# A two-layer encoder trunk on one core: one sigmoid, the heads' weight rests and x1's transposes put in a given order, x1's first tile scaled out of its PSUM bank, and half of tiles three and four scaled by ScalarE

## The chip, the cores and the metric

The program runs on one core of a Trainium2 chip. A core has five engines that this text speaks of: TensorE (PE in the profile; PEld is its weight load), VectorE (DVE), ScalarE (ACT), GpSimd (POOL) and SyncE (SP), which here only issues DMAs. Each engine takes its instructions in the order in which they were written into its queue; they wait for one another by semaphores. The metric is the device time of one execution in microseconds, less is better. The kernel before takes 660.94 us, the median of 3 runs (660.82 to 661.03).

## The reference

The trunk has two layers over 512 tokens of width 1024. Cut to what matters here:

```python
def rmsnorm(x, g):
    y = x * lax.rsqrt(jnp.mean(x * x, axis=-1, keepdims=True) + EPS)
    return y * g

for i in range(2):
    xn = rmsnorm(x, norm_g[i])
    y = mixer_na(xn, ...) if i == 0 else mixer_mla(xn, ...)
    h = x + y
    gate = jax.nn.sigmoid(rmsnorm(h, ple_norm[i]) @ ple_w_gate[i])
    x = h + gate * (p[i] @ ple_w_proj[i])
return rmsnorm(x, final_norm)
```

`mixer_na` is neighbourhood attention over a token grid. `mixer_mla` projects xn to a compressed query `c_q` (384 columns), a compressed key and value `c_kv` (256) and a rotary key part (32), normalises both, widens them to 16 heads of 96 query and key columns (64 without position, 32 rotary) and 64 value columns, and attends densely. Both mixers are multiplied by a SiLU gate before their output projection.

## The kernel before

Tokens lie in four tiles of 128 rows, t = 0 to 3; a tile has two halves of 512 columns, n (or g) = 0 and 1. Every fp32 product is made of three matmuls: each operand is split into a rounded main part ("hi") and the rest ("lo"), and hi·hi, lo·hi and hi·lo are added. For a weight, ScalarE makes the main part with a copy (`whi`, `wwhi`) and GpSimd the rest by a subtraction (`wlo`, `wwlo`; lines 83, 84, 583, 585); the raw weight comes by a DMA from SyncE's queue into one of three buffers (`wraw`). For an activation, ScalarE copies the transposed tile out of PSUM and VectorE subtracts (`split`, lines 94 and 96).

The program is written as one stream of calls. A scheduler of the compiler gives each engine its order by a timeline of its own, as far as data allows; `self.tc.issue_after(ins)` holds the instructions of a block behind `ins` where both are on the same engine, and adds no wait between engines.

Two stretches matter.

**From layer 0's gate to layer 1's compression.** `gate_seven` computes the gate product as seven block products instead of eight (block order 1, 7, 2, 6, 5, 3, 4; `p` in the code), each of two times 12 matmuls (i = 0, 1). Several products use one PSUM bank one after another: 6, 5 and 3 add up in a bank of tag T, 7 and 4 in one of tag S. After 6, ScalarE copies the bank to `s6` (L649 `s`), before 5 may add to it. `finish` applies the sigmoid (L592), multiplies by the projected embedding `pe` (L600) and adds to the residual tile `res[t]` (L602, `r`). Product 2 finishes tiles 0 and 1, half 0; 5 finishes tiles 2 and 3, half 1; 3 finishes tiles 0 and 1, half 1; 4 finishes tiles 2 and 3, half 0. Then `done` runs for the half: sum of squares (L1057), mean `mn` (L1058), and, once both halves are there, `rs` = mean^-0.5 on GpSimd (L1063), x1's scaling r · rs · gn on VectorE (L1071, `x1n`; gn is the norm's gain), four transposes a half on TensorE (L139), and the split into `x1h` and `x1l`. `mla_c` multiplies x1's tiles by the compression weights: part 0 with 384 columns, part 1 with 288, each in four chunks of k, 24 matmuls a tile and part (L107), and copies the results out (L685, `c`).

**The heads of layer 1.** `mla_heads` runs 64 steps of scores; the pair of heads j takes eight steps. For the next pairs it prepares rotary queries every second pair: `rope` ends with the main part `rh` (ScalarE, L771) and the rest `rl` (GpSimd, L772), which DMAs of SyncE's queue move into the query tiles `qe` and `qo`. GpSimd also normalises each step's exponentials (L830, `ex`) and makes the rests of the weights to come.

Of the kernel before, what the change touches and what calls it, by code (L numbers as in the profile page):

```python
# [16 lines left out]
ALU = mybir.AluOpType  # L17
# [3 lines left out]
S = 512  # L21
# [19 lines left out]
class Trunk:  # L41
# [522 lines left out]
    def gate_seven(self, pool, layer, rh, res, after):  # L564
# [22 lines left out]

        behind, loaded = [], self.last_load

        def finish(t, n, ps, o=0, wd=S, last=False):  # L590
# [10 lines left out]
            r = res[t][:, n * S + o:n * S + o + wd]  # L601
            (nc.vector if last else nc.gpsimd).tensor_tensor(out=r, in0=r, in1=x, op=ALU.add)  # L602
            if layer == 0 and last and (t, n) not in ((0, 0), (1, 0)):
                after(t, n, o, wd)
            else:
                behind.append(lambda: after(t, n, o, wd))
# [12 lines left out]
        for k, p in enumerate(order):  # L619
# [7 lines left out]
            for i in range(2):  # L627
                for o, wd in halves if i and p in (7, 4) else ((0, S),):
                    c = slice(o, o + wd)
                    if p in banks:  # L630
# [3 lines left out]
                         for c in range(2) for s, r in ((0, 0), (1, 0), (0, 1)) for k in (2 * c, 2 * c + 1)]  # L634
                    for j, (l, r) in enumerate(m):
                        with self.tc.issue_after(mm.ins):
                            mm = nc.tensor.matmul(ps, l, r, start=j == 0 and p in banks,  # L637
                                                  stop=j == 11 and p in (2, 3, 4), skip_group_check=True)
# [8 lines left out]
                    elif p == 6:  # L647
                        s6[i] = self.temp("s6")
                        copy = nc.scalar.activation(s6[i], ps, AF.Copy)  # L649
                        if i:  # L650
                            prep(order[-1], copy)
# [3 lines left out]
                    elif p == 5:  # L655
                        q = self.psum("mm" if i else "T")
                        sub(q, ps, s17[i])
                        sub(ps, ps, s1[i])
                        finish(2 + i, 1, q, last=layer == 0)
                    elif p == 2:  # L660
                        finish(i, 0, ps, last=True)
                    elif p == 3:
                        finish(i, 1, ps, last=True)
                    else:
                        finish(2 + i, 0, ps, o, wd, True)
# [3 lines left out]
    def mla_c(self, pool, xT, cT, sets):  # L669
# [47 lines left out]
    def mla_heads(self, pool, xT, cT, sets, oT):  # L717
# [32 lines left out]
        def load_qr(g, after=None):  # L750
            load(("qr", g), a["mla_qr"][g], 384, after)

# [103 lines left out]
        def pieces(j):  # L856
# [87 lines left out]
    def run(self):  # L944
# [64 lines left out]
        for layer in range(2):  # L1009
            with tc.tile_pool(name=f"out{layer}", bufs=4, reuse_waits="tile") as pool:  # L1010
# [38 lines left out]
                if layer == 0:  # L1049
                    mean = {}  # L1050

                    def done(t, n, o, w):
# [4 lines left out]
                        nc.scalar.activation(sq, r[:, n * S:(n + 1) * S], AF.Square, accum_out=ss)  # L1057
# [5 lines left out]
                        nc.gpsimd.tensor_tensor(out=rs, in0=mn, in1=self.half, op=ALU.pow)  # L1063
                        nc.gpsimd.tensor_scalar(self.rows[1][0][:, t:t + 1], mn, 1.0, None, op0=ALU.add)
                        nc.sync.dma_start(self.spill[t], r)
                        if not x1T:
                            x1T.extend([[self.bigtile(f"x1{s}{g}") for g in range(2)] for s in "hl"])
                        xn = pool.tile([P, D], F32, name="x1n", tag="xn", bufs=2)
                        for g in range(2):
                            c = slice(g * S, (g + 1) * S)  # L1070
                            nc.vector.scalar_tensor_tensor(xn[:, c], r[:, c], rs, gn[:, c], op0=ALU.mult, op1=ALU.mult)  # L1071
# [148 lines left out]
```

## Time and profile before

| what | us |
|---|---|
| median of 3 runs | 660.94 |
| the profiled execution's own time | 660.64 |
| its span in the trace | 658.4 |
| PE busy | 647.0 (98%) |
| POOL busy | 432.7 (66%) |
| ACT busy | 439.1 (67%) |
| DVE busy | 402.1 (61%) |

Times in the trace count from the start of the span. A busy PE is not PE at its peak, since matmuls overlap and their ends are modelled; what a stretch takes is better read from the starts of its instructions. In the rows of a timeline the columns are start, length, engine, line, operation, out<-in, shape and count, and in brackets how long the engine had been idle and for whom.

### The profile page before, as it was taken

The page shows a single profiled execution, that of the slowest core. Times are in us where ns is not written, and L with a number is a line of the kernel's source. Part 1 is how long each engine was busy: PE and PEld are TensorE (multiplying, and loading weights), DVE is VectorE, ACT ScalarE, POOL GpSimd, SP SyncE. Part 2 cuts the span into 40 slices and gives each one's busy share as a digit, 9 for nine tenths or more (in the row PEclk, how much of TensorE's full clock was granted, in tenths as well). Part 3 has the DMA queues.
Part 4 walks back from the last instruction along what each step waited for, and adds up shares of the span by engine and source line. Part 5 has one row for each costly group of instructions (what it writes and reads, how often), then busy time and mean ns, then how long its engine had stood idle before and what let it go on. Part 6 is the DMA issues. An engine that isn't in the chain of part 4 may idle for free.

```text
span 658.4 us, 10122 instructions
## 1 busy us (share of the span) xinstructions
PE 647.0 (98%) x3419; PEld 550.6 (84%) x3419; DVE 402.1 (61%) x856; ACT 439.1 (67%) x875; POOL 432.7 (66%) x381
## 2 busy tenths in 40 slices
PE   9999999999999999999999999999999999999994
PEld 6888888998988888887899888888888888888884
DVE  6290365845656516568834613888888886474855
ACT  7672586767767743787543635897979897537945
POOL 0495475895685673787554526785959878436974
PEclk9999999999999999999999999999999999999998
DMA  9944354987575989444733334120212213583524
GB/s 320 354 143 147 98 198 122 250 221 166 190 175 181 199 192 348 157 155 158 246 86 118 103 102 148 53 76 6 64 52 66 66 65 128 205 306 128 171 86 159
DMA packets 44755, 102.18 MB, mean 155 GB/s; under 512 B 4640, under 2 KB 17696, under 8 KB 44704
## 3 DMA queue, kind: packets, MB, share of 16 engines
q1 hardware_dynamic: 33776, 83.97, 38.0%
q0 software_dynamic: 10496, 16.78, 11.7%
q10 hardware_dynamic: 432, 0.79, 0.3%
q8 instruction: 27, 0.44, 0.3%
q14 instruction: 24, 0.20, 0.1%
HBM read 89.99 MB, written 25.17 MB: 175 GB/s over the span
## 4 chain that ended last, share of the span: by engine, by line
PE 92%; DVE 2%; ACT 2%; DMA 1%; issue 1%; POOL 1%; POOLq 0%; ACTq 0%
PE ps_mm L107 35%; PE ps_S L107 13%; PE ps_mm L734 7%; PE ps_T L139 6%; PE ps_O L845 5%; PE ps_T L637 4%; PE ps_T L107 3%; PE ps_O L107 3%; PE ps_T L238 2%; PE ps_O L400 2%; PE ps_S L637 2%; PE ps_mm L637 2%; PE ps_mm L184 2%; PE ps_T L388 2%; PE ps_S L352 1%; PE ps_S L351 1%
## 5 line engine op out<-in xcount | busy, mean ns | idle before, releaser
L84 POOL TENSOR_TENSOR wwlo<-wraw,wwhi 128x1024 fp32r<-128x1024 f32 (+5 forms) x78 | 143.3, 1852 | 74.7 <-ACT wwhi L83 53.2
L83 ACT ACTIVATE wwhi<-wraw 128x1024 fp32r<-128x1024 f32 (+5 forms) x81 | 65.5, 832 | 57.3 <-issue 19.2
L585 POOL TENSOR_TENSOR wlo<-wraw,whi 128x512 fp32r<-128x512 f32 x56 | 74.0, 1356 | 24.7 <-ACT whi L583 14.9
L830 POOL TENSOR_TENSOR ex<-ex,rc 128x512 f32<-128x512 f32 x64 | 66.1, 1043 | 25.1 <-DVE rc L829 18.1
L828 ACT ACTIVATE ex<-ps_S,mx 128x512 f32<-128x512 f32 x64 | 44.0, 687 | 12.1 <-DVE mx L826 11.1
L826 DVE TENSOR_REDUCE mx<-ps_S 128x1 f32<-128x512 f32 x64 | 43.7, 682 | 7.1 <-PE ps_S L107 6.5
L96 DVE TENSOR_TENSOR pt_lo<-ps_T,pt_hi 128x512 fp32r<-128x512 f32 x64 | 43.2, 681 | 7.6 <-ACT pt_hi L94 7.3
L374 POOL TENSOR_TENSOR ex<-ex,rc 128x128 f32<-128x128 f32 (+1 forms) x64 | 36.0, 619 | 15.0 <-DVE rc L370 15.0
L94 ACT ACTIVATE pt_hi<-ps_T 128x512 fp32r<-128x512 f32 x64 | 37.7, 594 | 4.2 <-PE ps_T L139 3.9
L107 PE MATMUL ps_mm<-xh,wwhi 128*128 128x512 f32 x152 | 40.3, 398 | 0.0
L107 PE MATMUL ps_mm<-xl,wwhi 128*128 128x512 f32 x152 | 38.4, 391 | 0.0
L139 PE MATMUL ps_T<-ident,ex 128*128 128x128 f32 x256 | 38.4, 272 | 0.0
L107 PE MATMUL ps_mm<-xh,wwlo 128*128 128x512 f32 x152 | 38.2, 391 | 0.0
L139 PEld LDWEIGHTS ps_T<-ident,ex 128*128 128x128 f32 x256 | 31.4, 140 | 7.7 <-POOL ex L830 0.4
L107 PEld LDWEIGHTS ps_mm<-xh,wwlo 128*128 128x128 f32 x152 | 28.3, 188 | 5.9
L107 PEld LDWEIGHTS ps_mm<-xl,wwhi 128*128 128x128 f32 x152 | 28.3, 188 | 5.7
L583 ACT ACTIVATE whi<-wraw 128x1024 fp32r<-128x1024 f32 x28 | 29.2, 1055 | 4.9 <-DMA wraw<-sum 2.7
L205 DVE TENSOR_TENSOR u<-ps_O,u 64x512 f32<-64x512 f32 x32 | 22.0, 687 | 17.2 <-ACT u L204 16.7
L368 ACT ACTIVATE ex<-ex,mx 128x128 f32<-128x128 f32 (+1 forms) x64 | 30.3, 476 | 2.7 <-DVE mx L358 1.8
L209 POOL TENSOR_TENSOR u<-u,z 128x512 f32<-128x512 f32 x16 | 21.9, 1368 | 15.2 <-DVE u L205 10.0
L107 PEld LDWEIGHTS ps_mm<-xh,wwhi 128*128 128x128 f32 x152 | 27.3, 188 | 4.8
L107 PE MATMUL ps_S<-ke,qe 96*128 96x512 f32 x96 | 29.0, 408 | 0.3 <-DMA qe<-rl 0.3
(432 smaller groups left out, 1847.0 us busy)
## 6 DMA issues: line engine op xcount, KB each, us to landing
sum<-gate POOLq DMA_DIRECT2D x12, 1024.0 KB, 8.2
wraw<-na_qk SPq DMA_DIRECT2D x16, 512.0 KB, 3.3
wraw<-sum SPq DMA_DIRECT2D x16, 512.0 KB, 3.3
pe<-pe SPq DMA_DIRECT2D x31, 256.0 KB, 6.4
wraw<-gate SPq DMA_DIRECT2D x12, 512.0 KB, 3.3
wraw<-na_v SPq DMA_DIRECT2D x8, 512.0 KB, 4.1
sum<-sum POOLq DMA_DIRECT2D x4, 1024.0 KB, 10.7
wraw<-na_o SPq DMA_DIRECT2D x8, 512.0 KB, 4.4
```

Source lines behind the costliest of these rows:

```text
L83: nc.scalar.activation(hi[:, c], raw[:, c], AF.Copy)
L84: f = lambda e, c=c: e.tensor_tensor(out=lo[:, c], in0=raw[:, c], in1=hi[:, c].bitcast(F32), op=ALU.subtract)
L94: self.last_copy = nc.scalar.activation(hi, src, AF.Copy, scale=scale)
L96: nc.vector.tensor_tensor(out=lo, in0=src, in1=hi.bitcast(F32), op=ALU.subtract)
L107: last = self.last_mm = nc.tensor.matmul(out, l, r, start=i == 0, stop=i == n - 1)
L139: self.last_mm = self.nc.tensor.transpose(t[:, i * P:(i + 1) * P], b, self.ident)
L585: nc.gpsimd.tensor_tensor(out=lo[:, o], in0=raw[:, o], in1=hi[:, o].bitcast(F32), op=ALU.subtract)
L637: mm = nc.tensor.matmul(ps, l, r, start=j == 0 and p in banks, stop=j == 11 and p in (2, 3, 4), skip_group_check=True)
L734: self.last_mm = nc.tensor.matmul(PS[key], *terms[i], start=i == 0, stop=i == len(terms) - 1)
L826: nc.vector.reduce_max(mx, sp, axis=AX.X, negate=True)
L828: nc.scalar.activation(ex, sp, AF.Exp, bias=mx, accum_out=sm)
L830: nc.gpsimd.tensor_tensor(out=ex, in0=ex, in1=rc.to_broadcast([P, S]), op=ALU.mult)
```

## The change

- In `gate_seven`, the finish of product 2's second tile (t = 1, half 0) is kept back until ScalarE has copied product 6's first bank to `s6`. Before, its sigmoid could stand ahead of that copy.
- For tile 0, half 1, VectorE's last add of `finish` writes to the PSUM bank instead of to `r`. The squares and the scaling read that bank; ScalarE copies it to `r` for the spill to memory. Half 0 of tile 0 is multiplied by the gain on VectorE early, and ScalarE applies `rs` to it.
- For tiles 2 and 3, half 1 is multiplied by the gain on GpSimd (`xg`) as soon as it is there, and ScalarE applies `rs`.
- x1's transposes get fixed places in TensorE's queue: tile 0's eight ahead of the last six matmuls of product 4, tile t+1's ahead of the second half of tile t's matmuls of part 0. GpSimd's rest of part 0's third weight chunk is put behind tile 0's `rs`.
- In `mla_heads`, the rests of the next rotary query weights, and in one pair those of the embedding `pT`, are put behind `rl` of the pair on GpSimd.

```diff
-        behind, loaded = [], self.last_load
+        behind, kept, loaded = [], [], self.last_load
...
-            (nc.vector if last else nc.gpsimd).tensor_tensor(out=r, in0=r, in1=x, op=ALU.add)
+            held = ps if layer == 0 and (t, n) == (0, 1) else r
+            (nc.vector if last else nc.gpsimd).tensor_tensor(out=held, in0=r, in1=x, op=ALU.add)
             if layer == 0 and last and (t, n) not in ((0, 0), (1, 0)):
-                after(t, n, o, wd)
+                after(t, n, o, wd, held)
...
+                        if layer == 0 and (p, i, j) == (4, 1, 6):
+                            mm = self.turned[0]
                         with self.tc.issue_after(mm.ins):
...
                         copy = nc.scalar.activation(s6[i], ps, AF.Copy)
+                        if kept:
+                            with self.tc.issue_after(copy.ins):
+                                finish(*kept.pop(), last=True)
...
+                    elif p == 2 and i and layer == 0:
+                        kept.append((i, 0, ps))
...
-            ws = [self.load_w(a["mla_c"][part][c], 2 * wn, extra=c == 3) for c in range(4)]
+            ws = []
+            for c in range(4):
+                with self.tc.issue_after(self.power.ins) if (part, c) == (0, 2) else nullcontext():
+                    ws.append(self.load_w(a["mla_c"][part][c], 2 * wn, extra=c == 3))
...
-                self.mms(ps[:, :wn], self.by_chunk(lambda s, k: L(xT[s], k, t), W))
+                m = self.by_chunk(lambda s, k: L(xT[s], k, t), W)
+                for j, (l, r) in enumerate(m):
+                    with self.tc.issue_after(self.turned[t + 1].ins) if (part, j) == (0, 12) and t < 3 else nullcontext():
+                        mm = nc.tensor.matmul(ps[:, :wn], l, r, start=j == 0, stop=j == 23)
...
-        def load(key, ap, n, after=None):
+        def load(key, ap, n, after=None, rests=None):
             with self.tc.issue_after((A.get(after) or self.last_copy).ins) if after else nullcontext():
-                W_[key] = self.load_w(ap, n, parts=2)
+                with self.tc.issue_after(A[rests].ins) if rests else nullcontext():
+                    W_[key] = self.load_w(ap, n, parts=2)
...
-                add(2, *((load_qr, g + 1, ("q", n)) if j < 5 else (load, "p", a["pT"][1], 1024, ("q", n))))
+                add(2, *((load_qr, g + 1, ("q", n), ("rl", g)) if j < 5 else
+                         (load, "p", a["pT"][1], 1024, ("q", n), ("rl", g))))
...
+                        half = r[:, n * S:(n + 1) * S] if held is None else held
+                        nc.scalar.activation(sq, half, AF.Square, accum_out=ss)
                         if t not in mean:
                             mean[t] = mn
+                            if t > 1:
+                                ahead[t, n] = self.temp("xg")
+                                nc.gpsimd.tensor_tensor(out=ahead[t, n], in0=r[:, n * S:(n + 1) * S],
+                                                        in1=gn[:, n * S:(n + 1) * S], op=ALU.mult)
                             return
...
+                        if t == 0:
+                            self.power = power
...
+                        if t == 0:
+                            nc.scalar.activation(r[:, S:], half, AF.Copy)
...
+                        if t == 0:
+                            ahead[t, 0] = xn[:, :S]
+                            nc.vector.tensor_tensor(out=xn[:, :S], in0=r[:, :S], in1=gn[:, :S], op=ALU.mult)
                         for g in range(2):
                             c = slice(g * S, (g + 1) * S)
-                            nc.vector.scalar_tensor_tensor(xn[:, c], r[:, c], rs, gn[:, c], op0=ALU.mult, op1=ALU.mult)
+                            if (t, g) in ahead:
+                                nc.scalar.activation(xn[:, c], ahead[t, g], AF.Copy, scale=rs)
+                            else:
+                                nc.vector.scalar_tensor_tensor(xn[:, c], r[:, c] if t else half, rs, gn[:, c],
+                                                               op0=ALU.mult, op1=ALU.mult)
...
+                        self.turned[t] = self.last_mm
```

The scheduler makes these orders of it. On TensorE, from the last 18 matmuls of product 4 (`ps_S<-..,X`) into part 0 of the compression (`ps_mm<-..,x1h` and `x1l`), the queue before and then now:

```order
L637 MATMUL ps_S<-whi,X_2977 128x512 x4
L637 MATMUL ps_S<-wlo,X_2977 128x512 x2
L637 MATMUL ps_S<-whi,X_2977 128x512 x4
L637 MATMUL ps_S<-wlo,X_2977 128x512 x2
L139 MATMUL ps_T<-ident,x1n 128x128 x12
L107 MATMUL ps_mm<-wwhi,x1h_3364 128x384 x4
L139 MATMUL ps_T<-ident,x1n 128x128 x4
L107 MATMUL ps_mm<-wwhi,x1l_3366 128x384 x2
```

```order
L640 MATMUL ps_S<-whi,X_2977 128x512 x4
L640 MATMUL ps_S<-wlo,X_2977 128x512 x2
L139 MATMUL ps_T<-ident,x1n 128x128 x8
L640 MATMUL ps_S<-whi,X_2977 128x512 x4
L640 MATMUL ps_S<-wlo,X_2977 128x512 x2
L698 MATMUL ps_mm<-wwhi,x1h_3369 128x384 x2
L698 MATMUL ps_mm<-wwhi,x1l_3371 128x384 x2
L698 MATMUL ps_mm<-wwlo,x1h_3369 128x384 x2
```

Tile 0's eight transposes moved ahead of six matmuls of product 4, and no transposes stand between a tile's first `x1h` matmuls and its `x1l` matmuls there.

On GpSimd, in the same place (`wlo`: product 4's weights; `wwlo`: part 0's; `rs`: tile 0's power first), before and then now:

```order
L585 TENSOR_TENSOR wlo<-wraw,whi 128x512 x14
L84 TENSOR_TENSOR wwlo<-wraw,wwhi 128x768 x3
L1063 TENSOR_TENSOR rs<-mn,half 128x1
L1064 TENSOR_SCALAR rowa_80<-mn 128x1
L1063 TENSOR_TENSOR rs<-mn,half 128x1
```

```order
L585 TENSOR_TENSOR wlo<-wraw,whi 128x512 x14
L84 TENSOR_TENSOR wwlo<-wraw,wwhi 128x768
L1080 TENSOR_TENSOR xg<-r,gn 128x512
L84 TENSOR_TENSOR wwlo<-wraw,wwhi 128x768
L1080 TENSOR_TENSOR xg<-r,gn 128x512
L1084 TENSOR_TENSOR rs<-mn,half 128x1
L1087 TENSOR_SCALAR rowa_80<-mn 128x1
L84 TENSOR_TENSOR wwlo<-wraw,wwhi 128x768
```

One weight rest left the front of tile 0's `rs`, and two multiplications by the gain came to stand there.

On SyncE, the moves of the last pairs' rotary queries (`mla_o` is a weight of the output projection), before and then now:

```order
L101 DMA qe_3528<-rh 32x512
L82 DMA wraw<-mla_o 128x1024
L101 DMA qo_3530<-rh 32x512
L101 DMA qe_3521<-rl 32x512
L101 DMA qo_3523<-rl 32x512
```

```order
L101 DMA qe_3534<-rh 32x512
L101 DMA qe_3527<-rl 32x512
L101 DMA qo_3529<-rl 32x512
L101 DMA qe_3535<-rl 32x512
L101 DMA qo_3536<-rh 32x512
```

The first move of `rl` went ahead of the weight and of a move of `rh`.

More of the change, by code (lines that the diff above doesn't have):

```diff
@@ L743, in k_terms, with load_qr @@
             return [(W(r, k), (ch, cl)[s][:, 3 + k, :]) for s, r in ((0, 0), (1, 0), (0, 1)) for k in range(2)]
-        def load(key, ap, n, after=None):
+        def load(key, ap, n, after=None, rests=None):
             with self.tc.issue_after((A.get(after) or self.last_copy).ins) if after else nullcontext():
-                W_[key] = self.load_w(ap, n, parts=2)
-        def load_qr(g, after=None):
-            load(("qr", g), a["mla_qr"][g], 384, after)
+                with self.tc.issue_after(A[rests].ins) if rests else nullcontext():
+                    W_[key] = self.load_w(ap, n, parts=2)
+        def load_qr(g, after=None, rests=None):
+            load(("qr", g), a["mla_qr"][g], 384, after, rests)
         def load_kv(g, after=None):
@@ L1049, in run, with done @@
                 if layer == 0:
-                    mean = {}
-                    def done(t, n, o, w):
+                    mean, ahead, self.turned = {}, {}, {}
+                    def done(t, n, o, w, held=None):
                         r = res[t]
@@ L1056, in done @@
                         mn = self.small.tile([P, 1], F32, name="mn", tag="mn")
-                        nc.scalar.activation(sq, r[:, n * S:(n + 1) * S], AF.Square, accum_out=ss)
+                        half = r[:, n * S:(n + 1) * S] if held is None else held
+                        nc.scalar.activation(sq, half, AF.Square, accum_out=ss)
                         nc.vector.tensor_scalar(mn, ss, 1.0 / D, mean.get(t, EPS), op0=ALU.mult, op1=ALU.add)
@@ L1060, in done @@
                             mean[t] = mn
+                            if t > 1:
+                                ahead[t, n] = self.temp("xg")
+                                nc.gpsimd.tensor_tensor(out=ahead[t, n], in0=r[:, n * S:(n + 1) * S],
+                                                        in1=gn[:, n * S:(n + 1) * S], op=ALU.mult)
                             return
                         rs = self.small.tile([P, 1], F32, name="rs", tag="rs")
-                        nc.gpsimd.tensor_tensor(out=rs, in0=mn, in1=self.half, op=ALU.pow)
+                        power = nc.gpsimd.tensor_tensor(out=rs, in0=mn, in1=self.half, op=ALU.pow)
+                        if t == 0:
+                            self.power = power
                         nc.gpsimd.tensor_scalar(self.rows[1][0][:, t:t + 1], mn, 1.0, None, op0=ALU.add)
+                        if t == 0:
+                            nc.scalar.activation(r[:, S:], half, AF.Copy)
                         nc.sync.dma_start(self.spill[t], r)
```

## The prediction

> **What bounds the kernel.** I read the page first, then TensorE's waits, then the timelines of every engine around the few places where TensorE stood still.
>
> ```profile
> PE 647.0 (98%) x3419; PEld 550.6 (84%) x3419; DVE 402.1 (61%) x856; ACT 439.1 (67%) x875; POOL 432.7 (66%) x381
> ```
>
> TensorE's queue is the bound. The change removes no matmul, so it can gain only where TensorE waits. The waits that the change touches, the last of them at a weight load (total, times, longest):
>
> ```profile
> PE ps_T L637 <- ACT s L649: 0.6, 1, 0.6
> ...
> PE ps_mm L107 <- ACT x1h L94: 0.4, 1, 0.4
> ...
> PEld ps_S L107 <- DMA qe<-rl: 1.0, 2, 0.8
> ```
>
> The view counts only gaps between modelled ends, so I take each loss from the starts in TensorE's timeline:
>
> ```profile
> 304.43 0.61 PE L637 MATMUL ps_T<-wlo,X 128*128 128x512 f32 x2
> 305.66 1.20 PE L637 MATMUL ps_T<-whi,X 128*128 128x512 f32 x4 [0.61 <-ACT s L649]
> ...
> 320.75 1.07 PE L637 MATMUL ps_S<-whi,X 128*128 128x512 f32 x4
> ...
> 322.12 1.47 PE L139 MATMUL ps_T<-ident,x1n 128*128 128x128 f32 x12
> 323.55 0.62 PE L107 MATMUL ps_mm<-wwhi,x1h 128*128 128x384 f32 x2
> ...
> 332.26 0.62 PE L107 MATMUL ps_S<-wwhi,x1h 128*128 128x384 f32 x2
> ...
> 343.53 0.43 PE L107 MATMUL ps_T<-wwhi,x1h 128*128 128x288 f32 x2
> ...
> 356.09 0.81 PE L139 MATMUL ps_T<-ident,cn 128*128 128x128 f32 x6
> ```
>
> and the pace of undisturbed work from the chain of waits:
>
> ```profile
> 316.83 5.46 PE ps_S L637 x24
> ...
> 325.57 5.56 PE ps_mm L107 x32
> ...
> 356.25 0.66 PE ps_T L139 x6
> ```
>
> A 512-column matmul takes 5.46/24 = 0.2275 us, a 384-column one 5.56/32 = 0.174, a transpose 0.66/6 = 0.11. From these, the three losses:
>
> Loss 1, the `s` copy: after 304.43 two matmuls are due to end at 304.885, and product 5 starts at 305.66: 0.775 us.
>
> Loss 2, x1's transposes: from 322.12 to 343.53 are 21.41 us for 32 transposes and 96 matmuls of part 0, 32 x 0.11 + 96 x 0.174 = 20.2: 1.2 us. From 343.53 part 1 runs at an even pace.
>
> Loss 3 is in the heads:
>
> ```profile
> 517.91 0.71 PE L107 MATMUL ps_S<-ke,qe 96*128 96x512 f32 x2
> 518.97 0.50 PE L107 MATMUL ps_S<-ke,qe 96*128 96x512 f32 x1 [0.34 <-DMA qe<-rl]
> 519.30 0.40 PE L734 MATMUL ps_mm<-cT,wwhi 128*128 128x512 f32 x1
> ...
> 525.85 0.95 PE L107 MATMUL ps_S<-ke,qe 96*128 96x512 f32 x3
> 526.63 1.09 PE L734 MATMUL ps_mm<-cT,wwhi 128*128 128x512 f32 x4
> ```
>
> A step's three score matmuls behind transposes take 0.78 us (525.85 to 526.63), here 1.39: 0.61 us. The other of the two weight-load waits is 1.0 - 0.8 = 0.2 us, at an earlier pair; I count half of it. Together 0.7. All that the change can win is 0.775 + 1.2 + 0.7 = 2.7 us.
>
> **The sigmoid.** ScalarE's queue ahead of product 5:
>
> ```profile
> 303.61 0.64 ACT L592 ACTIVATE ps_mm<-ps_mm,rs 128x512 f32<-128x512 f32 x1
> 304.40 0.63 ACT L1057 ACTIVATE sq<-r 128x512 f32<-128x512 f32 x1
> ...
> 305.03 1.06 ACT L649 ACTIVATE s<-ps_T 128x512 f32<-128x512 f32 x2
> ```
>
> Both `s` copies stood behind the sigmoid and a square, though product 6's first bank was ready 12 x 0.2275 = 2.7 us before 304.9. Now the first copy takes the place at 303.61 and ends near 304.2, 0.7 ahead of need. The second follows sigmoid and square at about 305.3 to 305.9; product 5's second half needs it 2.7 us after 304.9. So 0.775 is won whole, and everything on TensorE to product 4 moves forward by as much. The price is a sigmoid later by half a microsecond, and one multiplication more on VectorE (x1n from r and gn, near 305). Each is hidden: VectorE's next work for TensorE is on product 5's first bank, which ends near 307.9. Bounds of the term: 0 if another operand came last, 0.775; I take 0.775.
>
> **x1's first tile.** The eight transposes now stand where the row at 320.75 stood, which becomes 320.75 - 0.775 = 319.98: 2.1 us sooner than 322.12. Both halves of x1n must be there by then, or everything behind in TensorE's queue waits, product 4's last six matmuls too. When are they? GpSimd first:
>
> ```profile
> 307.17 5.05 POOL L585 TENSOR_TENSOR wlo<-wraw,whi 128x512 fp32r<-128x512 f32 x4 [3.25 <-issue]
> 312.19 3.66 POOL L84 TENSOR_TENSOR wwlo<-wraw,wwhi 128x768 fp32r<-128x768 f32 x2
> 316.73 1.84 POOL L84 TENSOR_TENSOR wwlo<-wraw,wwhi 128x768 fp32r<-128x768 f32 x1 [0.88 <-ACT wwhi L83]
> 318.53 0.55 POOL L1063 TENSOR_TENSOR rs<-mn,half 128x1 f32<-128x1 f32 x1
> ```
>
> The chain to 312.19 stays, since it hangs on ScalarE's copies behind the second `s`, which move little. Then come two weight rests (3.66) and two `xg`. No GpSimd product r·gn is in the trace; the nearest row is its 128x512 operation on three SBUF tiles in `rope`:
>
> ```profile
> L770 POOL TENSOR_TENSOR rl<-rh,rl x4: 1289/1296/1306, 402.7 to 508.1; 128x512 f32<-128x512 f32 x4
> ```
>
> Two at about 1.27: 312.19 + 3.66 + 2.54 = 318.4, then `rs` ends at 318.95. That is as late as before (318.53 + 0.55 = 319.08), because two `xg` cost what one weight rest and its wait did. The bounds of an `xg` are 1.02 (half of the two `ex` in a row below) and 1.84 (a longer weight rest), so `rs` could end between 318.5 and 320.1.
>
> ScalarE then scales half 0. Ahead of it stands product 4's first sigmoid:
>
> ```profile
> 315.81 0.85 ACT L83 ACTIVATE wwhi<-wraw 128x768 fp32r<-128x768 f32 x1 [0.36 <-DMA wraw<-mla_c]
> ...
> 317.18 0.64 ACT L592 ACTIVATE ps_T<-ps_T,rs 128x512 f32<-128x512 f32 x1
> ...
> 322.32 0.66 ACT L592 ACTIVATE ps_S<-ps_S,rs 128x512 f32<-128x512 f32 x1 [1.69 <-PE ps_S L637]
> ```
>
> The sigmoid at 322.32 began 0.2 us after product 4 left TensorE at 322.12. The first half of product 4 ends 320.75 - 6 x 0.2275 - 0.775 = 318.6, its sigmoid runs 318.8 to 319.45, and the scaling, about 0.63 like the square above, ends near 320.05. Half 1 is scaled on VectorE out of PSUM. In front of it, ScalarE's copy to `r` (0.53, half of the two `s` above) pushes the sigmoid of 317.18 to 317.7; it ends at 318.35. VectorE multiplies, adds and scales, 0.7 to 0.75 each as in the `x1n` row below, to 320.5. The transposes of half 1 are due at 319.98 + 0.44 = 320.42. So tile 0 is late by about 0.1 us, and `rs` has half a microsecond of slack in front of ScalarE.
>
> **The later tiles.** With the transposes from 320.1, tile 0's part 0 begins at 320.1 + 0.88 + 6 x 0.2275 = 322.35. I carried each engine's new order forward, with about 0.6 us for ScalarE's and 0.7 us for VectorE's operations on 512 columns. Tile 0's `x1l` half 0 is ready near 322.4 (needed 322.7). GpSimd's third weight rest ends near 320.95, `rs` of tile 1 at 322.45, x1n of tile 1 at 323.85 (needed 324.4 for half 0, 324.9 for half 1). Tile 2 is ready at 325.9 (needed 326.35); its second transposes need the bank that VectorE leaves at 327.05 (needed 327.1). Tile 3 is ready at 329.2, needed 332.4. The fourth weight chunk is copied near 334.9 (needed 336.7). The slacks are 0.05 to 0.5 us, so I charge 0.15 for all later tiles beside the 0.1 for tile 0: of 1.2 us, 0.95 is won. Part 1 and the z products behind it keep their operands early: their weight copies hang on TensorE itself, and move with it.
>
> A price for going wrong here: VectorE's scaling meets GpSimd on the same memory.
>
> ```profile
> L1071 DVE SCALAR_TENSOR_TENSOR x1n<-r,rs,gn 128x512 f32<-128x512 f32 x8 | 5.6, 747 | 0.0
> ...
> L128 DVE SCALAR_TENSOR_TENSOR cn<-c,rs,gq 128x384 f32<-128x384 f32 x1 | 1.8, 1847 | 0.7 <-POOL rs L123 0.7
> ```
>
> The same operation with fewer elements took 1.85 instead of 0.75 us beside GpSimd's weight rests. Tile 0's half 1 now comes from PSUM; tile 1 has both tensor inputs in SBUF, but its `rs` stands behind the third weight rest on GpSimd, which is then idle, so I charge nothing. If it met one, x1n of tile 1 would come 1.1 us later, 0.6 beyond its slack. [...]
>
> **The heads.** GpSimd and SyncE ahead of the wait at 518.97:
>
> ```profile
> 510.37 2.55 POOL L84 TENSOR_TENSOR wwlo<-wraw,wwhi 128x512 fp32r<-128x512 f32 x2
> 512.88 2.04 POOL L830 TENSOR_TENSOR ex<-ex,rc 128x512 f32<-128x512 f32 x2
> 514.87 1.30 POOL L772 TENSOR_TENSOR rl<-rl,rh 128x512 fp32r<-128x512 f32 x1
> ```
>
> ```profile
> 514.17 0.63 SPq L101 DMA_DIRECT2D qe<-rh  x1
> 514.89 0.53 SPq L82 DMA_DIRECT2D wraw<-mla_o  x1
> 516.08 0.51 SPq L101 DMA_DIRECT2D qo<-rh  x1
> 516.69 0.54 SPq L101 DMA_DIRECT2D qe<-rl  x1
> ```
>
> Without the two weight rests ahead of it, `rl` ends by about 514.1 instead of 516.2 (the second `ex` waits for its reciprocal, so 2.1 is won rather than 2.55). `qe<-rl` now follows the row at 514.17 directly: 514.89 instead of 516.69, so it lands 1.8 us sooner, against the 0.61 missing. The wait goes, and 0.7 is won with the smaller one. The price: the two rests (2.55) run after `rl`, to 516.65, and the `ex` behind them begins half a microsecond later than the 516.17 at which `rl` ended before. A step's `ex` is transposed three steps after its scores (`turn(i - 3)`), which covers that; without this cover TensorE would lose the half microsecond. `mla_o` and `pT` come later by a few DMAs, far from their use.
>
> **The sum.** 0.775 + 0.95 + 0.7 = 2.4 us. The profiled execution took 660.64 for a span of 658.4, its median stands 0.3 above it at 660.94. So the changed kernel should come out at 660.94 - 2.4 = 658.5 us.
>
> **Rivals.**
>
> *A, late tiles.* The fixed places of the transposes cost what they free: TensorE reaches each tile before its x1n, by 0.2 to 0.5 us at a time (the slacks above are that small). Then loss 2 stays, and 0.775 + 0.7 remain: 659.5. Against it: VectorE and ScalarE idle at these places in the carried order.
>
> *B, the heads only pay elsewhere.* `rl` is early but another move or a late `ex` holds the scores, and only the gate's end gains: 660.94 - 1.7 = 659.2. Against it: the 1.8 us against 0.61.
>
> *C, nothing.* Product 5 waits for another operand and the tiles are late: within 0.2% (1.3 us, about what a measurement here tells from no change), near 660.4.
>
> *D, slower.* Tile 0's transposes, put into the middle of product 4, stop TensorE until `rs` is there. Tile 3's last sigmoid, `rs` and x1n come from the matmuls behind them, so a stall is not made up. Every us by which `rs` ends beyond 319.4 is lost whole; from 2.4 on the gain is gone, from 3.7 it is slower by 0.2%. That needs two `xg` of 2.5 us and more, or a third weight chunk that arrives as late. With both `xg` at the upper bound (1.84) the loss is 0.7, which gives 659.2; a loss of 4.5 would give 663.
>
> **Chances.** My forecast 0.55 (its own range 658.0 to 659.0), A 0.18, B 0.08, C 0.1, D 0.09. Faster by more than 1.3 us are the forecast, B and nearly all of A: 0.79; same 0.12; slower 0.09. The range runs from 657.7 (all 2.7 us won, and half a microsecond of spread) to 660.5; above it lie D and a little of C.
>
> **What would show it.** Right: no wait of product 5 for the `s` copy; about 34.4 us from tile 0's first transposes to those of `cn` (32 x 0.11 + 6 x 0.2275 + 96 x 0.174 + 12.56 + 0.25); no wait for `qe<-rl`. Wrong: a gap ahead of the transposes of x1n with GpSimd's `rs` or ScalarE's scaling as its end; a wait of part 0 for `x1l`; a score waiting for `qe` or transposes waiting for `ex` after 510.

## The result and the profile after

The changed kernel takes 657.94 us, the median of 6 runs (657.81 to 658.27); the kernel before took 660.98 beside it (660.81 to 661.04). The ratio is 0.9955 with a 95% interval of 0.9943 to 0.9968: 3.0 us faster, by the interval 2.1 to 3.8. The profiled execution took 657.81 us for a span of 655.9, 2.5 us less than the span before.

The page's busy times, and the waits of TensorE (whole span) and of its weight load (290 to 600 us), in the kernel after:

```profile
PE 646.3 (99%) x3419; PEld 551.1 (84%) x3419; DVE 399.5 (61%) x854; ACT 441.6 (67%) x879; POOL 433.9 (66%) x383
...
PE ps_T L972 <- PEq L1242: 0.8, 1, 0.8
...
PEld ps_T L640 <- ACT X L533: 0.5, 1, 0.5
PEld ps_T L139 <- ACT x1n L1100: 0.5, 1, 0.5
PEld ps_T L640 <- DVE X L534: 0.4, 1, 0.4
```

The same matmuls run, and the three waits that the prediction named are gone; what the first view has left is the wait at the kernel's start. One new row stands at the weight load: x1's transposes wait for ScalarE's scaling.

TensorE's timeline at the rows that answer to those of before (start of product 5 and its next block, tile 0's transposes, part 1's first matmuls, `cn`'s transposes):

```profile
304.41 0.62 PE L640 MATMUL ps_T<-wlo,X 128*128 128x512 f32 x2
304.87 1.07 PE L640 MATMUL ps_T<-whi,X 128*128 128x512 f32 x4
...
306.23 1.07 PE L640 MATMUL ps_T<-whi,X 128*128 128x512 f32 x4
...
319.38 0.61 PE L640 MATMUL ps_S<-wlo,X 128*128 128x512 f32 x2
320.02 1.09 PE L139 MATMUL ps_T<-ident,x1n 128*128 128x128 f32 x8
...
341.71 0.43 PE L698 MATMUL ps_T<-wwhi,x1h 128*128 128x288 f32 x2
...
354.48 0.82 PE L139 MATMUL ps_T<-ident,cn 128*128 128x128 f32 x6
```

Product 5 starts 0.79 us sooner, with no gap. One block of six matmuls further on it is 0.92 us ahead, since the kernel before took longer for the first block behind its wait (305.66 to 307.15, 1.49 us) than the kernel after (1.36):

```profile
307.15 1.07 PE L637 MATMUL ps_T<-whi,X 128*128 128x512 f32 x4
```

Tile 0's transposes were due two matmuls behind 319.38, at 319.835, and start 0.185 late. Part 1 of the compression starts 1.82 us sooner (341.71; before: 343.53), and `cn` is reached 1.61 us sooner.

The other engines there (ScalarE, then VectorE, then GpSimd):

```profile
303.56 0.58 ACT L652 ACTIVATE s<-ps_T 128x512 f32<-128x512 f32 x1
...
305.22 0.59 ACT L652 ACTIVATE s<-ps_T 128x512 f32<-128x512 f32 x1
...
319.25 0.71 ACT L1100 ACTIVATE x1n<-x1n,rs 128x512 f32<-128x512 f32 x1
```

```profile
318.95 0.74 DVE L1102 SCALAR_TENSOR_TENSOR x1n<-ps_T,rs,gn 128x512 f32<-128x512 f32 x1
```

```profile
316.77 1.30 POOL L1080 TENSOR_TENSOR xg<-r,gn 128x512 f32<-128x512 f32 x1
318.01 0.57 POOL L1084 TENSOR_TENSOR rs<-mn,half 128x1 f32<-128x1 f32 x1
```

The first `s` copy ends at 304.14, 0.7 us ahead of need. `rs` ends at 318.58, half 1 is scaled by 319.69 and half 0 by 319.96: it is ScalarE's half that holds the transposes.

The heads, at the place of the old wait for `qe<-rl` (TensorE, GpSimd, SyncE):

```profile
516.23 0.94 PE L107 MATMUL ps_S<-ke,qe 96*128 96x512 f32 x3
517.01 0.39 PE L748 MATMUL ps_mm<-cT,wwhi 128*128 128x512 f32 x1
```

```profile
511.28 1.30 POOL L787 TENSOR_TENSOR rl<-rl,rh 128x512 fp32r<-128x512 f32 x1
512.53 2.55 POOL L84 TENSOR_TENSOR wwlo<-wraw,wwhi 128x512 fp32r<-128x512 f32 x2
```

```profile
512.16 0.53 SPq L101 DMA_DIRECT2D qe<-rh  x1
512.79 0.54 SPq L101 DMA_DIRECT2D qe<-rl  x1
```

The three scores take 0.78 us instead of 1.39, the two weight rests follow `rl`, and `qe<-rl` is issued right behind `qe<-rh`.

**Where the time came from.** A start of the timeline says by how much TensorE is ahead of the kernel before. Profiled executions are shifted against each other by up to 0.4 us from their start on; I take the row `ps_mm<-wlo,X` at 294.28 (before) as zero and subtract its shift (after: 294.26, so 0.02). The table gives the lead in us so worked out, at `cn`'s transposes (before: 356.09), at the matmuls of `cT` behind the scores that wait for `qe<-rl` (481.23 and 519.30), at a product of the projected embedding in the heads (542.79), and at the last matmul row (649.45). The last column is the ratio of the times with its interval. One of the ten executions of the kernel with the third rest ahead of `rs` took 1683 us, which no trace explains, and its ratio leaves that one out.

| kernel | cn | 481 | 519 | 543 | end | ratio |
|---|---|---|---|---|---|---|
| the whole change | 1.59 | 1.67 | 2.27 | 2.60 | 2.62 | 0.9955 (0.9943 to 0.9968) |
| sigmoid alone | 0.58 | 0.24 | 0.18 | 0.16 | 0.18 | 0.9992 (0.9983 to 1.0001) |
| heads alone | 0.01 | 0.08 | 0.68 | 1.01 | 1.02 | 0.9984 (0.9975 to 0.9994) |
| x1 alone | 0.75 | 0.61 | 0.86 | 0.83 | 0.85 | 0.9987 (0.9977 to 0.9996) |
| all but the heads | 1.64 | 1.51 | 1.78 | 1.74 | 1.76 | 0.9973 (0.9962 to 0.9983) |
| all, no fixed places | -1.73 | -1.66 | -1.06 | -0.73 | -0.72 | 1.0002 (0.9993 to 1.0012) |
| all, x1 scaled as before | 0.06 | 0.13 | 0.73 | 1.06 | 1.06 | 0.9985 (0.9976 to 0.9994) |
| third rest ahead of `rs` | 0.19 | 0.26 | 0.86 | 1.21 | 1.21 | 0.9978 (0.9968 to 0.9988) |
| transposes six matmuls sooner | 0.20 | 0.26 | 0.86 | 1.18 | 1.19 | 0.9982 (0.9973 to 0.9991) |
| transposes one matmul later | 1.72 | 1.79 | 2.38 | 2.74 | 2.75 | 0.9956 (0.9941 to 0.9970) |
| tile 0's place alone | 1.72 | 1.78 | 2.39 | 2.72 | 2.73 | 0.9956 (0.9941 to 0.9971) |

In the whole change 0.77 us come from the start of product 5 (305.66 - 304.87 - 0.02), 0.82 more are there at `cn`, 0.08 at the earlier pair, 0.60 at the later one, and 0.33 between 519 and 543, which the prediction had not named.

### The profile page after: what moved, and what is told of

It reads as the page before. It is cut to its first block, busy times and chain, and to the rows that moved or that the text cites. A ratio compares the mean times of both kernels' runs of the same rounds, so it can differ in the third digit from the quotient of the medians.

```text
span 655.9 us, 10127 instructions
## 1 busy us (share of the span) xinstructions
PE 646.3 (99%) x3419; PEld 551.1 (84%) x3419; DVE 399.5 (61%) x854; ACT 441.6 (67%) x879; POOL 433.9 (66%) x383
## 4 chain that ended last, share of the span: by engine, by line
PE 93%; DVE 2%; ACT 1%; DMA 1%; issue 1%; POOL 1%; POOLq 0%; ACTq 0%
PE ps_mm L107 34%; PE ps_S L107 12%; PE ps_mm L748 7%; PE ps_T L139 6%; PE ps_T L640 5%; PE ps_O L860 5%; PE ps_T L107 3%; PE ps_T L238 2%; PE ps_O L400 2%; PE ps_O L107 2%; PE ps_S L640 2%; PE ps_mm L698 2%; PE ps_mm L640 2%; PE ps_mm L184 2%; PE ps_T L388 2%; PE ps_S L698 1%
## 5 line engine op out<-in xcount | busy, mean ns | idle before, releaser
L107 PE MATMUL ps_S<-ko,qo 128*128 128x512 f32 x96 | 28.9, 409 | 0.0
```

The source lines that it names most:

```text
L107: last = self.last_mm = nc.tensor.matmul(out, l, r, start=i == 0, stop=i == n - 1)
```

## The experiments

### Each part alone

The kernel before with one part of the change. The sigmoid:

```diff
+                        if kept:
+                            with self.tc.issue_after(copy.ins):
+                                finish(*kept.pop(), last=True)
...
+                    elif p == 2 and i and layer == 0:
+                        kept.append((i, 0, ps))
```

> The kernel before with only the sigmoid of product 2's second tile kept back behind the first s copy. Separate terms (mine): product 5 starts at 304.9 instead of 305.66, the wait for s is gone, and nearly all of it lasts to the transposes of cn: 660.2 to 660.4 us. Rival (terms not separate: x1's tiles, whose rs stands behind three weight rests on GpSimd, do not move with it): the wait for s goes and the 0.78 us come back as longer waits for x1h or x1n: 660.8 to 661.0.

The heads:

```diff
-                add(2, *((load_qr, g + 1, ("q", n)) if j < 5 else (load, "p", a["pT"][1], 1024, ("q", n))))
+                add(2, *((load_qr, g + 1, ("q", n), ("rl", g)) if j < 5 else
+                         (load, "p", a["pT"][1], 1024, ("q", n), ("rl", g))))
```

> The kernel before with only the heads' weight rests put behind rl. Mine: the waits for qe<-rl go, 0.7 us; the 0.35 us that the changed kernel wins beside that near 530 to 538 (a transpose that waited for ex) come with it, since the orders of ScalarE and VectorE there changed with the weight rests: 659.9 to 660.1. Rival (the 0.35 us come only from the earlier time at which TensorE reaches the place, after the gate's gain): 660.3.

x1's part (the places, `xg`, the PSUM bank, the third rest behind `rs`), with the sigmoid and the heads as before; shown is what is taken back of the changed kernel:

```diff
-                        if kept:
-                            with self.tc.issue_after(copy.ins):
-                                finish(*kept.pop(), last=True)
...
-                    elif p == 2 and i and layer == 0:
-                        kept.append((i, 0, ps))
...
-                with self.tc.issue_after(A[rests].ins) if rests else nullcontext():
-                    W_[key] = self.load_w(ap, n, parts=2)
+                W_[key] = self.load_w(ap, n, parts=2)
```

> The kernel before with only x1's part: the scaling out of PSUM and by ScalarE, xg on GpSimd, the third weight rest behind rs, and the transposes in their places. Mine: from tile 0's transposes to those of cn about 34.5 us as in the changed kernel, the wait for s stays at 0.6; 0.8 us won: 660.1 to 660.2. Rival (x1's part only pays because the sigmoid came first): under 0.3 us won, 660.7 to 660.9.

They took 660.07, 659.60 and 659.77 us (the kernel before, beside them: 660.65). Each part gains, as the first expectation of each said and its rival did not, but at TensorE's end in other sizes than the prediction's sum had: the heads 1.02 us instead of 0.7, the sigmoid 0.18 instead of 0.78, and x1 0.85. Each lead is that of one execution. By the middle of the spans of all ten executions (the kernel before: 658.6, of 31) the heads win 1.1, x1 0.85 and the sigmoid 0.7 (657.9), so it is the sigmoid's trace that shows less than its kernel mostly wins; its ratio's interval reaches 1.

The heads' surplus lies between 519 and 543, at the transposes of exponentials and the scores behind them. TensorE in the kernel before, then in the kernel with the heads' part alone:

```profile
533.97 0.60 PE L139 MATMUL ps_T<-ident,ex 128*128 128x128 f32 x4
534.49 0.95 PE L107 MATMUL ps_S<-ko,qo 128*128 128x512 f32 x3
...
537.56 0.40 PE L734 MATMUL ps_mm<-wwlo,wwhi 128*128 128x512 f32 x1
537.93 0.66 PE L139 MATMUL ps_T<-ident,ex 128*128 128x128 f32 x4
```

```profile
533.37 0.60 PE L139 MATMUL ps_T<-ident,ex 128*128 128x128 f32 x4
533.73 0.95 PE L107 MATMUL ps_S<-ko,qo 128*128 128x512 f32 x3
...
536.80 0.39 PE L734 MATMUL ps_mm<-wwlo,wwhi 128*128 128x512 f32 x1
537.03 0.60 PE L139 MATMUL ps_T<-ident,ex 128*128 128x128 f32 x4
```

From the transposes to the next scores it was 0.52 us and is 0.36, and from the last `pT` matmul to the transposes 0.37 and 0.23: together 0.30 of the 0.33. In the kernel before both are waits at a weight load (290 to 600 us), which the kernel with the heads' part doesn't have:

```profile
PEld ps_T L139 <- POOL ex L830: 0.4, 1, 0.4
PEld ps_S L107 <- ACT ex L828: 0.2, 1, 0.2
```

Before, GpSimd ran `u` ahead of the exponentials at the second place; with the heads' part it runs an exponential first:

```profile
535.59 1.28 POOL L209 TENSOR_TENSOR u<-u,z 128x512 f32<-128x512 f32 x1 [1.67 <-DVE u L205]
536.84 3.04 POOL L830 TENSOR_TENSOR ex<-ex,rc 128x512 f32<-128x512 f32 x3
```

```profile
534.56 1.04 POOL L831 TENSOR_TENSOR ex<-ex,rc 128x512 f32<-128x512 f32 x1 [1.19 <-DVE rc L830]
535.56 1.29 POOL L209 TENSOR_TENSOR u<-u,z 128x512 f32<-128x512 f32 x1
536.81 1.04 POOL L831 TENSOR_TENSOR ex<-ex,rc 128x512 f32<-128x512 f32 x1
```

ScalarE does the same at the first place: its copy `u` stood ahead of the exponentials (533.04 and 533.65), and stands behind them now (533.30 and 532.50). The scheduler gave these engines another order once the rests had moved. Whether the rests of the rotary query weights or those of `pT` brought it was not tried apart.

The sigmoid alone wins its 0.75 at product 5 (305.66 - 304.78 - 0.13), and in its own trace gives most of it back. At the weight load of this kernel, 290 to 600 us:

```profile
PEld ps_S L107 <- DMA qe<-rl: 1.4, 2, 0.8
...
PEld ps_T L139 <- DVE x1l L96: 0.8, 2, 0.4
```

Both rows stood at 1.0 and 0.4 before. x1's transposes in the old order wait twice for `x1l`, which leaves 0.58 at `cn`, and the earlier pair's wait for `qe<-rl` grows, which leaves 0.24 in this execution.

### Does the wait for `qe<-rl` eat what is won ahead of it?

The single leads add to 2.05 at the end, the whole has 2.62. The changed kernel with the heads' edit taken back:

```diff
-                add(2, *((load_qr, g + 1, ("q", n), ("rl", g)) if j < 5 else
-                         (load, "p", a["pT"][1], 1024, ("q", n), ("rl", g))))
+                add(2, *((load_qr, g + 1, ("q", n)) if j < 5 else (load, "p", a["pT"][1], 1024, ("q", n))))
```

> The changed kernel with the heads' weight rests back in their old order; the sigmoid and x1's parts stay. Measured one by one, the gains at TensorE's last matmuls, less each trace's shift at 294, were 0.18 us (the sigmoid alone), 0.85 (x1 alone) and 1.02 (the heads alone), 2.05 in all, where the three together won 2.62: 0.57 more. My theory: the gate's end wins 0.78 and 0.8 as it does in the whole change, but the rotary rest rl comes when GpSimd and SyncE bring it, not when TensorE is ready, so the waits for qe<-rl near 478 and 517 eat about a third of what was won ahead of them. Then cn's transposes come 1.6 us sooner than before, and by 542 about 1.0 us is left: a gain of 1.0 by span, near 659.8, with waits for qe<-rl of 1.5 us or more in all. Rival: the parts add up, and the 0.57 are the sigmoid's alone, since x1's transposes in the old order ate them at 340: then 2.62 - 1.02 = 1.6 are left at the end, near 659.2, with waits for qe<-rl as in the kernel before, 1.0 us.

It took 658.95 us (before: 660.62), with a lead of 1.64 at `cn` and 1.76 at the end. My theory falls: `rl` moves with TensorE (at the earlier pair it begins at 474.40 instead of 475.97, 1.57 sooner), and the wait for its move was no longer than before.

```profile
PEld ps_S L107 <- DMA qe<-rl: 0.9, 2, 0.5
```

The rival's numbers hold (1.6 at the end, 1.0 of waits), its reason only in part. Together the two have 1.76 at the end, one by one 0.18 + 0.85 = 1.03. A part of that is there at `cn`: 0.58 + 0.75 alone, 1.64 together. The rest is the sigmoid's trace at the earlier pair, where 0.34 went: there the `cT` matmul stood 3.86 us behind the issue of `qe<-rl` (477.00 to 480.86), in the kernel before 3.52 (477.71 to 481.23). The view of the tile `qe` shows why: from issue to landing that transfer took 3.5 us, in the kernel before 3.2. By the middle of the spans of all executions nothing is missing: this kernel wins 1.65 (658.5 less 656.85), the two alone 0.7 + 0.85 = 1.55. So the half microsecond was mostly one execution's.

The same view shows something that the heads' edit does at the earlier pair. Where SyncE issues two loads of `pT` ahead of the first `qe<-rl` (before, the sigmoid alone, x1 alone, this kernel), the transfer lands 3.2 to 3.5 us after its issue; where `pT` comes behind it (the whole change, the heads alone) it lands after 1.9.

### The fixed places

The changed kernel without the lines that put x1's transposes into TensorE's queue:

```diff
-                        if layer == 0 and (p, i, j) == (4, 1, 6):
-                            mm = self.turned[0]
...
-                    with self.tc.issue_after(self.turned[t + 1].ins) if (part, j) == (0, 12) and t < 3 else nullcontext():
+                    with nullcontext():
```

> The changed kernel without fixed places for the transposes; scaling, sigmoid and heads as changed. Mine (the places make the gain of 0.8 us, since a first x1h matmul without other work in between waits for ScalarE's and VectorE's split): waits of part 0 for x1h or x1l come back, 658.6 to 658.9. Rival (the earlier x1n makes it): 657.9 to 658.2.

It took 660.53 us (659.67 to 661.98), as much as before. Both expectations missed by about 2 us, though the waits that mine named did come. TensorE, 320 to 328 us:

```profile
322.67 0.65 PE L139 MATMUL ps_T<-ident,x1n 128*128 128x128 f32 x4 [0.68 <-DVE x1n L1100]
323.08 0.60 PE L696 MATMUL ps_mm<-wwhi,x1h 128*128 128x384 f32 x2
324.81 0.64 PE L696 MATMUL ps_mm<-wwhi,x1h 128*128 128x384 f32 x2 [1.13 <-ACT x1h L94]
...
326.02 0.99 PE L696 MATMUL ps_mm<-wwhi,x1l 128*128 128x384 f32 x2
326.81 0.84 PE L696 MATMUL ps_mm<-wwlo,x1h 128*128 128x384 f32 x2
```

Left to itself the scheduler put tile 1's first transposes ahead of tile 0's matmuls, where they wait for tile 1's x1n, and then the matmuls wait for ScalarE's copies. From tile 0's transposes (320.95) to `cn` (357.65) it takes 36.70 us, 2.24 more than in the changed kernel. And two matmuls, 0.35 us apart elsewhere, take 0.64 and more from 326 on. Busy times and the granted clock (PEclk) by windows of this kernel:

```profile
322.00:323.00 1.00, 0.33 (x3) 0.33 (x4) 1.00 (x2) 0.77 (x2) 0.96 (x1) 1.00 0.83 285
323.00:324.00 1.00, 0.68 (x5) 0.36 (x3) 1.00 (x3) 0.94 (x2) 0.36 (x2) 1.00 0.96 390
324.00:325.00 1.00, 0.19 (x1) 0.19 (x2) 1.00 (x2) 0.75 (x2) 0.00 (x0) 1.00 0.19 74
...
327.00:328.00 1.00, 1.00 (x5) 1.00 (x4) 0.99 (x3) 0.26 (x2) 0.78 (x3) 0.50 1.00 344
```

The first number behind the stretch is its length, the second TensorE's busy time, and the third from the right the clock. After 1.2 us of work in 3 us (322 to 325) the clock is halved (0.50) in this trace, from 325.3 to 328.7. Of this kernel's ten executions four have a mean clock of 0.992 or 0.993 and spans of 659.2 to 659.9, six have 0.995 to 0.997 and 657.8 to 658.5: by these spans the lower clock costs about 1.5 us when it comes, and without it the waits alone leave a gain of about half a microsecond at most.

Which of the places carries it? The changed kernel with tile 0's place kept and those of tiles 1 to 3 left to the scheduler:

```diff
-                    with self.tc.issue_after(self.turned[t + 1].ins) if (part, j) == (0, 12) and t < 3 else nullcontext():
+                    with self.tc.issue_after(self.turned[t + 1].ins) if (part, j) == (0, 12) and t < 0 else nullcontext():
```

> The changed kernel with tile 0's place alone given: the transposes of tiles 1 to 3 stand where the scheduler puts them, which moves one pair of matmuls, tile 1's second eight transposes standing two matmuls later. On the other engines nothing moves. Without any place 3.3 us were lost on TensorE by 356 (1.1 ahead of tile 0's transposes, 2.2 behind them, a good part of it at a halved clock). My theory: the loss comes from tile 0's place, which sets the whole order behind it; then this kernel's cn comes within 0.2 us of the changed kernel's 354.48, and the time is 657.8 to 658.1. Rival: the places of tiles 1 to 3 carry the 2.2 us behind tile 0's transposes: 659 to 660.2, with a wait for x1n or x1h between 322 and 340.

657.89 us, and `cn` at 354.36. My theory holds: tile 0's place is all that matters here, since the scheduler then finds nearly the same order for the other tiles.

### The scaling

The places kept, and x1 scaled on VectorE from SBUF as before, with no `xg` and no PSUM bank:

```diff
-            held = ps if layer == 0 and (t, n) == (0, 1) else r
+            held = r
...
-                            if t > 1:
-                                ahead[t, n] = self.temp("xg")
...
-                        if t == 0:
-                            ahead[t, 0] = xn[:, :S]
```

> The changed kernel with the fixed places, but x1 scaled as before: both halves of every tile on VectorE out of SBUF, no xg, no copy to r. Mine (scaling and places need each other): rs of tile 0 comes earlier, about 317.4, but VectorE's two scalings follow one another and meet GpSimd's third weight rest on the same memory, so tile 0's second half is ready near 320.6 and TensorE waits 0.3 to 0.8 us there or at a later tile: 658.2 to 658.8. Rival (the places alone do it, the scaling is hidden): 657.9 to 658.1.

659.68 us (before: 660.80), with nothing left at `cn` (0.06): x1's places with the old scaling lose what the sigmoid wins. My expectation named the collision and was 0.9 us too low; the rival missed by more. VectorE's scaling of tile 0, beside GpSimd's third weight rest, and the longest wait that follows on TensorE:

```profile
317.91 2.94 DVE L1093 SCALAR_TENSOR_TENSOR x1n<-r,rs,gn 128x512 f32<-128x512 f32 x2
```

```profile
317.81 1.83 POOL L84 TENSOR_TENSOR wwlo<-wraw,wwhi 128x768 fp32r<-128x768 f32 x1
```

```profile
328.89 0.66 PE L139 MATMUL ps_T<-ident,x1n 128*128 128x128 f32 x4 [0.59 <-DVE x1l L96]
```

Two scalings of 0.74 took 2.94 us, 1.5 more: the collision that the prediction priced at 1.1 (for tile 1) and kept out of the sum. VectorE's work behind it is late: tile 0's split begins at 322.82 (in the changed kernel at 321.35), and the second mean of tile 1 at 322.70 (320.93).

### What a late tile 0 costs

Rival D said that a stall at tile 0's transposes is lost whole. Two ways to make one: GpSimd's third weight rest ahead of `rs`, and the transposes six matmuls sooner. And one to take away what is left: one matmul later.

```diff
-                with self.tc.issue_after(self.power.ins) if (part, c) == (0, 2) else nullcontext():
+                with nullcontext():
```

> The changed kernel with the third weight rest back ahead of tile 0's rs on GpSimd (1.85 us). Mine (what rs comes late is lost whole, since TensorE's queue stands in the middle of product 4): rs ends near 320.4 instead of 318.58, tile 0's transposes start near 321.2 instead of 320.02, 1.1 to 1.2 us lost: 659.1. Rival (the queue behind makes it up by waits that get shorter): 658.0 to 658.3.

```diff
-                        if layer == 0 and (p, i, j) == (4, 1, 6):
+                        if layer == 0 and (p, i, j) == (4, 1, 0):
```

> The changed kernel with tile 0's transposes six matmuls sooner, ahead of the last twelve of product 4. Mine: x1n comes no sooner than before (ScalarE has product 4's first sigmoid in front), so the transposes still start near 320.0, with a wait of some 1.5 us in front, and the six matmuls that stood in that time come behind: 1.36 us lost, 659.3. Rival (work made up later): 658.0 to 658.5.

```diff
-                        if layer == 0 and (p, i, j) == (4, 1, 6):
+                        if layer == 0 and (p, i, j) == (4, 1, 7):
```

> The changed kernel with tile 0's transposes one matmul later (ahead of the last five). Mine: the wait of 0.2 us for x1n goes (due at 320.06, ready at 319.97), all else as before: the transposes of cn come 0.15 to 0.2 us sooner than 354.48, 657.8 us. Rival: a later tile was as late as the first, and nothing is won: 657.9 to 658.0.

They took 659.45, 659.53 and 657.79 us. GpSimd's `rs` and TensorE in the first, then TensorE in the second:

```profile
319.88 0.57 POOL L1084 TENSOR_TENSOR rs<-mn,half 128x1 f32<-128x1 f32 x1
```

```profile
321.26 1.34 PE L139 MATMUL ps_T<-ident,x1n 128*128 128x128 f32 x8 [1.24 <-ACT x1n L1100]
```

```profile
320.44 1.09 PE L139 MATMUL ps_T<-ident,x1n 128*128 128x128 f32 x8 [1.39 <-ACT x1n L1100]
```

In the first, `rs` begins 1.87 us later than in the changed kernel (318.01), the transposes 1.24 later, and `cn` 1.40 (1.59 - 0.19), 0.16 more than the stall. In the second the transposes wait 1.39 us, and `cn` comes 1.39 later. The stall is lost whole, and nothing behind it makes it up; my expectations were met to 0.4 us, the rivals, by which the later tiles' slack takes it, were not. One matmul later, `cn` comes 0.13 sooner and the end too, as expected of the 0.185 that tile 0 was late; the difference of the medians (0.15) is no more than their spread.

## Why the prediction was right

It said 658.5 us (657.7 to 660.5), faster; 657.94 was measured. By TensorE's rows 2.62 us were won where the sum had 2.4; the medians' 3.0 agrees within its interval. The waits and their causes were as forecast. That the sum came so near is in part luck: a gain that was not foreseen (0.33) covers a loss that was not foreseen (0.21).

- **The sigmoid**, 0.775: 0.77. The `s` copy stands where it was put and ends at 304.14 (said: near 304.2). The sigmoid alone shows the same 0.75 at that place. The term was a little small: one block further the lead is 0.90 (307.15 - 306.23 - 0.02), since before the change the block behind the wait took 1.49 us and now takes 1.36.
- **x1's first tile.** The chain came out as carried forward: an `xg` 1.30 (taken: 1.27), `rs` ends 318.58 (318.95), ScalarE's half 319.96 (320.05). VectorE's half was ready at 319.69, not 320.5, so ScalarE alone sets the start; it is 0.185 late where 0.1 was charged.
- **The later tiles**: this term was right, and a term behind it was missing. From tile 0's transposes to part 1's first matmul are 21.69 us (320.02 to 341.71), where the prediction's undisturbed work gives 21.59: 0.10 was lost where 0.15 was charged. By then the lead is 1.80 (343.53 - 341.71 - 0.02), 0.90 beyond the sigmoid's, where 0.95 was forecast.
- **Part 1** was taken to move as it was, 12.56 us. Its 96 matmuls now take 12.77 (341.71 to 354.48), and the 0.21 are lost: with them x1 has won 0.69 at `cn` (0.82 when the sigmoid is counted as 0.77). No wait stands in the views there; each matmul takes 0.133 us instead of 0.131. It is no accident of one execution: all eight kernels with tile 0's place have 12.75 to 12.77 us, the four without it 12.56. Why the place slows part 1 stays open. The check of "about 34.4 us" (34.46) came out so well because the prediction's 0.25 of lateness stands against 0.10 in the later tiles and 0.21 in part 1, where nothing had been charged.
- **The heads.** The later pair won 0.60 (said 0.61), the earlier 0.08 (0.1). The step that failed is the price, "the `ex` behind them begins half a microsecond later", which was thought to be covered and at best nothing: the new order of the engines won a further 0.33 at 530 to 538. I had looked only at what the move delays.
- **The rivals.** A: no wait for tiles 1 to 3 stands in the views. B and C: each of the three parts won something. D: its price was about right. With `rs` ending at 320.45, 1.05 us beyond the 319.4 named, the transposes came 1.24 later; the point from which it costs is thus 0.63 behind the measured end of `rs`, at 319.2. The two `xg` were not the danger: without the new scaling, or without the third rest's place, TensorE's fixed places lost 1.4 to 1.5 at `cn`, so the gain hangs on all three at once.
- **The collision** at VectorE was left out of the sum, rightly: tile 0's half 1, read from PSUM, was scaled in 0.74 us although GpSimd's third weight rest ran beside it (318.77, 1.85 us), and tile 1's halves, read from SBUF, in 0.70 us each (321.96 to 323.36), where GpSimd ran no rest. With the old scaling, from SBUF and beside that rest, the collision came, at 1.5 us: of the rest's 1.83 us, 1.73 were left when VectorE began, and its two scalings took 1.5 longer. What makes the two engines collide no run here tests.

## What to carry to other kernels

When the bound engine's queue is what is reordered, each moved block is as good as its latest operand: carry that operand's chain through every engine first, since a stall ahead of a block in the middle of the queue was lost whole (1.24 and 1.39 us). A place in one queue and the work that feeds it belong together: here, at `cn`, the places without the feeding won nothing, nor did the feeding without the places. And one trace is one execution: the sigmoid alone led by 0.18 us at the end of its trace, while the middle of ten spans puts it at 0.7, so look at all spans before explaining why parts don't add.

## What the hardware showed that was not expected

Two short waits of 0.68 and 1.13 us, which left TensorE 1.2 us of work in 3 us, were followed by a halved clock (0.50) for 3.4 us (325.3 to 328.7) in the trace of the kernel without fixed places. Four of its ten executions have the lower mean clock (0.992 or 0.993), and their spans are about 1.5 us longer; the place is known for the traced one alone. A single wait of 1.39 us, longer than either, shows nothing of the kind in the kernel with the transposes six matmuls sooner: the clock is 1.00 in its trace from 314 to 358, TensorE being busy for 2.62 us of the four from 318 to 322, and the mean clocks of its ten executions are 0.995 to 0.997. So beside the 1.8 us of waits stand, in the executions with the lower clock, 1.5 us more by the spans, nearly as much again. Whether the waits bring the lower clock, by what about them, and why in four executions of ten, no run here shows.
